# A two-layer hybrid encoder trunk: DeltaNet systems built one after each half projection, without TensorE transposes, and the triangular inverse written ahead of the mLSTM

## The chip, the cores and the metric

The kernel runs on one core of one Trainium2 chip. The metric is the device time of the whole program in microseconds (us), median of several runs. TensorE is PE in the profile (its weight loads PEld), VectorE DVE, ScalarE ACT, GpSimd POOL, and SyncE SP; SPq is the queue of DMA issues on SP.

## The reference

Input x is [1, 1024, 1024] in fp32. Two layers follow each other, each with an adaptive norm (`shift`, `scale`, `gate` from a matrix product of the conditioning vector with `ada_w`), one input projection, mixers and one output projection. The even layer's mixers are an mLSTM and a gated DeltaNet, each of four heads, forward and backward in time. Of the odd layer (convolution and dilated attention) nothing is changed. The DeltaNet part, where the change lies:

```python
a = strict_lower(beta * (k @ k^T) * exp(gc_i - gc_j))      # per chunk of 64 and head
tmat = a + eye
u = solve(tmat, beta * v);  w = solve(tmat, beta * exp(gc) * k)
attn = tril((q @ k^T) * exp(gc_i - gc_j))
for chunk in order:                                        # and once more, flipped in time
    v_new = u - w @ state
    o = (q * exp(gc)) @ state + attn @ v_new
    state = exp(gl) * state + (k * exp(gl - gc))^T @ v_new
```

## The kernel before, in words

All of x is held transposed, 128 rows by two halves of 512 tokens. A dense projection in fp32 is made of three matmuls in a reduced format: activations and weights are split in a high and a low part (`wsplit`: one load of 512 KB, a cast on ACT, a subtraction on POOL). `project` makes 128 output columns in two halves, and a half is 24 matmuls 128x512 (`prod`) into one of two PSUM banks set aside for that. These projections are named dq, dk, dv, mq, mk, mv, z.

**DeltaNet systems.** Time is cut in eight chunks of 128 tokens. `dn_system(ch)` makes the triangular system of a chunk, for four heads and two directions: four matmuls k·kᵀ into the bank KK (two such banks); a load of the table `gc_d` (cumulative log decays) spread over all 128 partitions; per direction a mask on POOL (L599), four exponentials on ACT (L624) and four multiplications on DVE (L647), and a store to `nd_d` in DRAM (L649). For the backward direction the blocks are transposed by TensorE into the bank NT (L158), copied by ACT (L655) and stored to `nt_d` (L656). All eight calls stand in a row in the program, ahead of the mlstm's buffers.

**Inverse.** `dn_inverse` loads the 64x64 blocks with one block in each partition, 64 for a direction (L675), inverts their 32x32 corners by 30 pairs of DVE steps (L681, L683), stores the result straight and with its axes swapped (ACT, L689), loads them as rows, and makes the corner blocks by products on PE (iG, iV, iT, with L706 on DVE ahead of the first). `dn_step`, the recurrence, reads what it stores: eight steps of two half-steps (one for each direction). A half-step is a chain of small matmuls (T1, T2, kS, Yr, qS, dS) with ACT and DVE between them. Where no projection is left to run beside it, PE waits in it.

**mLSTM.** `mlstm_weights(ch)` makes the scores S (PE, bank tag A), loads the table `nmu_d` spread over the partitions into E (L813), masks it, takes exponentials, multiplies by S (L818, DVE) and stores the product; `mlstm_step(j)` uses it. `m_k` also makes kw, keys by weights (L897).

**Beside it** runs `modulation`, a generator that reads `ada_w` piece by piece (L439 load of 256 KB, ACT L441, POOL L443); each `wsplit` moves it on by seven pieces, and after eight pieces PE sums the partitions (gps), with L456 on DVE behind.

**What sets the order.** The Tile framework's scheduler gives each engine one queue, filled in program order where nothing waits by its model; an engine runs its queue in order. `tc.issue_after(ins)` puts what is issued in it behind that instruction. The program's order is a list of steps, quoted with the change. After it come the recurrence with the rest of the projections, and the odd layer.

Of the kernel before, what the change touches and what calls it, by code (L numbers as in the profile page):

```python
# [9 lines left out]
F32 = mybir.dt.float32  # L10
# [7 lines left out]
P = 128  # L18
T = 1024
D = 1024  # L20
KT = 8
NCH = 8
# [34 lines left out]
def trunk(ctx, tc, x, c, norm_g, ada_w, ada_b, ev_w_in, ev_m_gate_b, ev_dn_dt_bias, ev_dn_a_log,  # L57
          ev_dn_conv_w, ev_m_norm_g, ev_dn_norm_g, ev_w_out, od_w_in, od_dw_w, od_dw_b, od_ln_g,
          od_ln_b, od_w_out, rel_bias, final_g, sel, onehot, seen, out):
    nc = tc.nc  # L60
# [8 lines left out]
    dr = pool("dr", 1, DRAM)  # L69
# [16 lines left out]
    def sl(off, *shape):  # L86
        return part_of(U, off, shape)

    def ring(off, n, *shape, of=None):

        size = 1
        for k in shape:
            size *= k
        i = 0
        while True:
            yield part_of(U if of is None else of, off + (i % n) * size, shape)
            i += 1
# [8 lines left out]
    def bank(name, shape=(P, 512), tag="t"):  # L106
        return psb.tile(list(shape), F32, tag=tag, name=name, bufs=BANKS[tag])
# [12 lines left out]
        tc.add_manual_dep(ins, first.name, mybir.DependencyInfo(mybir.DependencyClass.NoSync, mybir.DependencyReason.DATA),  # L120
                          reason="issue order")

    pace = {"gen": None, "n": 0}
    TICKS = 7
    uid = [0]

    def nm(s):
        uid[0] += 1
        return f"{s}_{uid[0]}"
# [26 lines left out]
    def tr(o, i):  # L156
        k = i.shape[0]
        nc.tensor.transpose(o, i, ident[:k, :k])  # L158
# [116 lines left out]
    def project(w, hT, name, use):  # L275
        for hf in range(2):
            ps = ibank(nm(name))
            prod(ps, w, hT[hf], range(KT))
            use(hf, ps)


    w0 = ev_w_in[0]
# [29 lines left out]
    def columns(g):  # L312
        for tiles, b0 in zip(ada[g], (2 * g, 8 + 2 * g)):
# [5 lines left out]
                          in_=wgr.rearrange("p k (g c) -> p k g c", g=4))  # L319
# [180 lines left out]
    cs1 = page("cs1", tag="a")  # L500
# [51 lines left out]
    nc.scalar.activation(out=wrow[0:8], in_=wrow[0:8], func=AF.Exp)  # L552
    nmu = cB
    nc.scalar.mul(out=nmu[0:8], in_=cs2[0:8], mul=-1.0)
    nmu_d = dr.tile([8, T], F32, name="nmu_d")
    wrow_d = dr.tile([8, T], F32, name="wrow_d")
    gc_d = dr.tile([8, T], F32, name="gc_d")
    wold_d = dr.tile([8, NCH], F32, name="wold_d")
    gl_d = dr.tile([8, NCH], F32, name="gl_d")
    nc.sync.dma_start(out=gc_d, in_=cs1[96:104])  # L560
    nc.sync.dma_start(out=nmu_d, in_=nmu[0:8])
    nc.sync.dma_start(out=wrow_d, in_=wrow[0:8])
    nc.sync.dma_start(out=wold_d, in_=wold)
    nc.sync.dma_start(out=gl_d, in_=tot[96:104])
# [1 line left out]
    for e in range(2):  # L566
        nc.sync.dma_start(out=woldb[e * 64:e * 64 + 64],
                          in_=wold_d.rearrange("(d q e) c -> e d q c", d=2, e=2)[e:e + 1].to_broadcast([64, 2, 2, NCH]))
# [6 lines left out]
    for src, dst in ((cs1, col1), (cs2, col2)):  # L575
        for q in range(2):
            b_ = turn(src, q)
            nc.vector.tensor_copy(out=dst[:, q * 4:q * 4 + 4, :].rearrange("p c (g r) -> p c g r", r=8),
                                  in_=b_.rearrange("p (c g r) -> p c g r", c=4, g=4)[:, :, :, 0:8])
# [20 lines left out]
                                channel_multiplier=cm_)  # L600

    def brow(src, d, ch):
        return src[4 * d:4 * d + 4, ch * P:(ch + 1) * P].rearrange("(o h) l -> o h l", o=1).to_broadcast([P, 4, P])

    cc = cst.tile([P, NCH, 8], F32, name="cc")
    ncc = cst.tile([P, NCH, 8], F32, name="ncc")
# [17 lines left out]
            nc.scalar.activation(out=B_[:, h, :], in_=B_[:, h, :], func=AF.Exp, bias=ngc[:, ch, 4 * d + h:4 * d + h + 1])  # L624

    nd_d = dr.tile([2, NCH, 4, P, P], F32, name="nd_d")
    nt_d = dr.tile([NCH, 4, P, P], F32, name="nt_d")

    xl_d = [dr.tile([2, 2, NCH, 4, 64, 64], F32, name=f"xl{i}_d") for i in range(2)]

    def etile(tag):
        return wk.tile([P, 4, P], F32, tag=tag, name=nm("E"), bufs=2)

    n_r, nt_r = ring(0, 4, 8, P), ring(4096, 2, 4, P)

    def dn_system(ch):
        tcs = slice(ch * P, ch * P + P)
        KK = bank(nm("KK"), (P, 4, P), "B")
        for h in range(4):
            mm(KK[:, h, :], kT[h][:, tcs], kT[h][:, tcs], True, True)  # L640
        B_ = next(n_r)
        nc.sync.dma_start(out=B_, in_=gc_d[:, tcs].rearrange("(o r) l -> o r l", o=1).to_broadcast([P, 8, P]))
        for d in range(2):
            decays(B_[:, 4 * d:4 * d + 4, :], d, ch)
            for h in range(4):
                u = 4 * d + h
                nc.vector.scalar_tensor_tensor(out=B_[:, u, :], in0=KK[:, h, :], scalar=ncc[:, ch, u:u + 1],  # L647
                                               in1=B_[:, u, :], op0=ALU.mult, op1=ALU.mult)
            nc.sync.dma_start(out=nd_d[d, ch].rearrange("h j i -> j h i"), in_=B_[:, 4 * d:4 * d + 4, :])  # L649

        ps = bank(nm("NT"), (P, 4, P), "A")
        for h in range(4):
            tr(ps[:, h, :], B_[:, 4 + h, :])
        Nt = next(nt_r)
        nc.scalar.copy(out=Nt, in_=ps)  # L655
        nc.sync.dma_start(out=nt_d[ch].rearrange("h i j -> i h j"), in_=Nt)  # L656

    def dn_inverse(n):

# [9 lines left out]
            return part_of(next(iv_r)[:, 0:n], 0, shape)  # L669

        sq = NL[:, 0:4096].rearrange("p (a b) -> p a b", b=64)
        for d, src in enumerate((nd_d[0], nt_d)):
            for b in range(2):
                bs = slice(64 * b, 64 * b + 64)
                nc.sync.dma_start(out=sq[64 * d + 32 * b:64 * d + 32 * b + 32],  # L675
                                  in_=src[:, :, bs, bs].rearrange("c h j i -> (c h) j i"))
        D2 = NL.rearrange("p (s x) -> p s x", s=2)[:, :, 0:2048].rearrange("p s (a b) -> p s a b", b=64)[:, :, :, 0:32]
        for k in range(30, 0, -1):
            m = 31 - k
# [23 lines left out]
        for ch in range(NCH):  # L703
# [3 lines left out]
            ps = bank(nm("iG"), (P, 4, 32), "C")  # L707
# [3 lines left out]
            ps = bank(nm("iV"), (P, 4, 32), "C")  # L711
# [78 lines left out]

    MARK = 1
    dn_scales()
    for ch in range(NCH):
        dn_system(ch)
    mq = [page(f"mq{j}", tag="a") for j in range(2)]
    mk = [page(f"mk{j}", tag="a") for j in range(2)]
    oml_d = dr.tile([NCH, P, 4, P], F32, name="oml_d")
# [124 lines left out]
                mlstm_weights(ch)  # L922
            mlstm_step(j)

    for step, n in ((dn_q, 0), (dn_v, 0), (m_q, 0), (dn_q, 1), (m_q, 1), (dn_q, 2), (dn_q, 3), (m_k, 1), (m_v, 0), (m_v, 2), (m_v, 3), (m_v, 1), (m_k, 0), (mlstm, 0), (dn_v, 1), (dn_inverse, 0), (gate_chunk, 0), (dn_v, 2), (gate_chunk, 1), (dn_v, 3)):
        step(n)
    Y_r, aux_r, ke_r, vv_r, v2_r = (ring(0, 2, 4, P), ring(1024, 2, 2, 4, 64), ring(2048, 2, 4, P), ring(3072, 3, 4, P),
                                    ring(5632, 2, 4, P))
# [677 lines left out]
```

## Time and profile before

| what | value |
|---|---|
| time of three runs | 1521.6, 1512.96, 1513.93 us; median 1513.93 |
| profiled execution | 1522.57 us, its span 1520.8 us |
| PE busy | 1344.9 us, 88% of the span |
| DVE, ACT, POOL busy | 879.0, 585.9, 460.4 us |
| granted TensorE clock, mean | 0.933 |

The span is what the profiler saw from the first to the last instruction. The granted clock is TensorE's, as a share of full speed: 1.00 is the upper of its two levels (2.4 GHz) all through a stretch, 0.50 the lower (1.2 GHz), and what lies between is a mixture. The program is one long PE queue with other engines beside it, so the stretches in which PE stands still or runs at the lower level are the ones to look at.

### The profile page before, as it was taken

To read this page: it belongs to the slowest core of one execution; us is meant where nothing else is said; L and a number is where in the kernel's file an instruction comes from. 1 tells how busy PE (TensorE), PEld (TensorE's weight loads), DVE (VectorE), ACT (ScalarE), POOL (GpSimd) and SP (SyncE) were. 2 spreads that over 40 slices of the span, in tenths; PEclk is the share of its full clock that TensorE was granted. 3 is DMA by queue.
4 is the path that set the end of the run, shared out by engine and by line. 5 is a ranking of instruction groups with operands and counts; after the bars stand their busy time and mean duration, and the time that the engine had idled before them with its cause. 6 is when DMAs were issued, how large, how long until landed. Compare 5 with 4: busy or idle time off the path is not lost. (4 is left out here: it accounts for less than half of the span.)

```text
span 1520.8 us, 20504 instructions
## 1 busy us (share of the span) xinstructions
PE 1344.9 (88%) x7331; PEld 1070.9 (70%) x7331; DVE 879.0 (58%) x1622; ACT 585.9 (39%) x1415; POOL 460.4 (30%) x357
## 2 busy tenths in 40 slices
PE   3978958878878988988999989889999999998998
PEld 2766746657667866777878857667776767876786
DVE  6789456933324641345854539998886454336334
ACT  5354454454444323343443321123324743326212
POOL 3454523444234511210234102322125233022210
PEclk9898987989899999889999999999999998997899
DMA  9334479369667785455655271010241233245322
GB/s 319 102 83 113 106 168 235 109 223 177 177 180 229 234 203 147 124 140 143 211 189 156 84 144 56 28 56 22 67 140 43 66 127 119 84 143 158 102 82 104
DMA packets 256456, 205.11 MB, mean 135 GB/s; under 512 B 59391, under 2 KB 219667, under 8 KB 256227
## 3 DMA queue, kind: packets, MB, share of 16 engines
q1 hardware_dynamic: 235555, 193.32, 45.1%
q10 hardware_dynamic: 20800, 10.49, 2.4%
q8 instruction: 58, 0.95, 0.3%
q14 instruction: 43, 0.35, 0.1%
HBM read 148.45 MB, written 58.98 MB: 136 GB/s over the span
## 5 line engine op out<-in xcount | busy, mean ns | idle before, releaser
L265 POOL TENSOR_TENSOR wlo<-wraw,whi 128x1024 fp32r<-128x1024 f32 x60 | 163.2, 2720 | 358.6 <-ACT whi L264 345.9
L1245 DVE SCALAR_TENSOR_TENSOR u<-xp,U,u 128x1009 f32<-128x1009 f32 (+14 forms) x120 | 176.2, 1502 | 1.0
L264 ACT CAST whi<-wraw 128x1024 fp32r<-128x1024 f32 x60 | 62.6, 1044 | 136.5 <-PE gb L139 49.1
L139 PE MATMUL z<-hhi,whi 128*128 128x512 f32 x256 | 108.1, 422 | 4.5 <-ACT mo L768 4.2
L139 PE MATMUL z<-hlo,whi 128*128 128x512 f32 x256 | 106.8, 417 | 0.0
L139 PE MATMUL z<-hhi,wlo 128*128 128x512 f32 x256 | 106.3, 415 | 0.0
L443 POOL TENSOR_TENSOR U<-U 128x512 f32<-128x512 f32 x56 | 79.4, 1419 | 76.9 <-ACT U L441 74.4
L139 PE MATMUL y<-wohi,mhi 128*128 128x512 f32 x240 | 97.9, 409 | 2.2 <-ACT mhi L1054 2.1
L139 PE MATMUL y<-wolo,mhi 128*128 128x512 f32 x240 | 96.8, 403 | 0.0
L139 PE MATMUL y<-wohi,mlo 128*128 128x512 f32 x240 | 96.1, 402 | 0.4 <-DVE mlo L1055 0.3
L441 ACT ACTIVATE U<-U,cs 128x512 f32<-128x512 f32 x64 | 45.9, 722 | 84.8 <-DMA U<-in_ada_w_dram 83.5
L599 POOL TENSOR_SCALAR_AFFINE_SELECT E<-E 128x512 f32<-128x512 f32 x32 | 21.4, 670 | 170.3 <-DMA E<-gc_d 71.3
L1397 DVE COPY U<-pT 128x512 f32<-128x512 f32 x48 | 32.5, 689 | 55.7 <-PE pT L158 55.6
L139 PEld LDWEIGHTS z<-hhi,whi 128*128 128x128 f32 x256 | 50.7, 198 | 16.7 <-ACT mo L768 4.6
L139 PEld LDWEIGHTS z<-hhi,wlo 128*128 128x128 f32 x256 | 50.5, 197 | 11.9 <-issue 1.1
L139 PEld LDWEIGHTS z<-hlo,whi 128*128 128x128 f32 x256 | 50.6, 197 | 11.3 <-issue 0.9
L139 PEld LDWEIGHTS y<-wohi,mhi 128*128 128x128 f32 x240 | 46.0, 192 | 13.5 <-ACT mhi L1054 2.5
L139 PE MATMUL sc<-ak,aq 128*128 128x256 f32 (+1 forms) x128 | 44.2, 429 | 11.6 <-DVE o L1372 9.8
L139 PEld LDWEIGHTS y<-wohi,mlo 128*128 128x128 f32 x240 | 45.9, 191 | 11.9 <-DVE mlo L1055 1.3
L1370 DVE CUSTOM_DVE_ANT_0 pt<-sc,U 128x256 f32<-128x256 f32 (+1 forms) x64 | 25.9, 404 | 48.6 <-PE sc L139 23.4
L139 PEld LDWEIGHTS y<-wolo,mhi 128*128 128x128 f32 x240 | 46.2, 193 | 10.3
L1374 ACT ACTIVATE pt<-pt,o 128x256 f32<-128x256 f32 (+1 forms) x64 | 31.4, 490 | 53.6 <-DVE o L1370 48.1
(455 smaller groups left out, 3603.7 us busy)
## 6 DMA issues: line engine op xcount, KB each, us to landing
wraw<-in_ev_w_in_dram SPq DMA_DIRECT2D x32, 512.0 KB
U<-in_ada_w_dram SPq DMA_DIRECT2D x64, 256.0 KB
wraw<-in_od_w_in_dram ACTq DMA_DIRECT2D x20, 512.0 KB
x<-in_x_dram SPq DMA_DIRECT2D x11, 512.0 KB
ada<-in_ada_w_dram SPq DMA_DIRECT2D x10, 512.0 KB
od_d<-o SPq DMA_DIRECT2D x64, 66.0 KB
U<-od_d SPq DMA_DIRECT2D x4, 1056.0 KB
U<-gc_d SPq DMA_DIRECT2D x8, 512.0 KB
```

The costliest lines, as they stand in the source:

```text
L139: return nc.tensor.matmul(o, lhsT=l, rhs=r, start=s, stop=e, skip_group_check=shared).ins
L264: nc.scalar.copy(out=hi, in_=raw)
L265: nc.gpsimd.tensor_tensor(out=lo, in0=raw, in1=f(hi), op=ALU.subtract)
L441: nc.scalar.mul(out=t_ if k else acc, in_=t_, mul=cs[:, k:k + 1])
L443: nc.gpsimd.tensor_tensor(out=acc, in0=acc, in1=t_, op=ALU.add)
L599: nc.gpsimd.affine_select(out=ap, in_=ap, pattern=[[0, 4], [pat, P]], compare_op=ALU.is_ge, fill=NEG, base=0, channel_multiplier=cm_)
L1245: nc.vector.scalar_tensor_tensor(out=y[:, lo:hi], in0=xp[:, lo + d:hi + d], scalar=w_, in1=y[:, lo:hi], op0=ALU.mult, op1=ALU.add)
L1370: nc.vector.tensor_tensor_reduce(out=x1_, in0=ps[:, c0:c1], in1=bias[:, e, c0:c1], scale=1.0, scalar=1e30, op0=ALU.add, op1=ALU.min, accum ...
L1374: nc.scalar.activation(out=x1_, in_=x1_, func=AF.Exp, scale=-1.0, bias=mn1, accum_out=o2[:, 0, 128 + e:129 + e])
L1397: nc.vector.tensor_copy(out=PT, in_=tb)
```

## The change

Four things change. (1) The eight `dn_system` calls no longer stand in a row. A new step `systems`, put behind the second mq projection, fills a list; `project` takes one system from it after each half projection and issues it behind that half's last matmul. (2) The backward transposes on PE, their copies on ACT and `nt_d` are gone. `dn_inverse` loads the backward blocks from `nd_d` in four rounds of two loads through one buffer `tmp`, and in each round a copy on ACT (64 partitions, 1024 elements in each) swaps the two axes of a block. The freed scratch space makes the ring of B_ five buffers instead of four. (3) The two tables `gc_d` and `nmu_d` are stored by chunk, so that what a load reads for one partition is one piece: 4 KB instead of eight of 512 B in `dn_system`, 2 KB instead of four of 512 B in the 32 loads of `brow` (16 of `nmu_d`, 16 of `gc_d`). (4) `dn_inverse` is written ahead of the mLSTM.

```diff
     def project(w, hT, name, use):
         for hf in range(2):
             ps = ibank(nm(name))
             prod(ps, w, hT[hf], range(KT))
             use(hf, ps)
+            if pace["sys"]:
+                with tc.issue_after(pace["mm"]):
+                    pace["sys"].pop(0)()
...
-    nmu_d = dr.tile([8, T], F32, name="nmu_d")
+    nmu_d = dr.tile([NCH, 8, P], F32, name="nmu_d")
...
-    gc_d = dr.tile([8, T], F32, name="gc_d")
+    gc_d = dr.tile([NCH, 8, P], F32, name="gc_d")
...
     def brow(src, d, ch):
-        return src[4 * d:4 * d + 4, ch * P:(ch + 1) * P].rearrange("(o h) l -> o h l", o=1).to_broadcast([P, 4, P])
+        return src[ch:ch + 1, 4 * d:4 * d + 4, :].to_broadcast([P, 4, P])
...
-    n_r, nt_r = ring(0, 4, 8, P), ring(4096, 2, 4, P)
+    n_r = ring(0, 5, 8, P)
...
-        nc.sync.dma_start(out=B_, in_=gc_d[:, tcs].rearrange("(o r) l -> o r l", o=1).to_broadcast([P, 8, P]))
+        nc.sync.dma_start(out=B_, in_=gc_d[ch:ch + 1].to_broadcast([P, 8, P]))
...
-        ps = bank(nm("NT"), (P, 4, P), "A")
-        for h in range(4):
-            tr(ps[:, h, :], B_[:, 4 + h, :])
-        Nt = next(nt_r)
-        nc.scalar.copy(out=Nt, in_=ps)
-        nc.sync.dma_start(out=nt_d[ch].rearrange("h i j -> i h j"), in_=Nt)
...
-        for d, src in enumerate((nd_d[0], nt_d)):
+        tmp = sl(4160, 16, 64)
+        for b in range(2):
+            bs = slice(64 * b, 64 * b + 64)
+            nc.sync.dma_start(out=sq[32 * b:32 * b + 32], in_=nd_d[0][:, :, bs, bs].rearrange("c h j i -> (c h) j i"))
+        for q in range(4):
             for b in range(2):
-                bs = slice(64 * b, 64 * b + 64)
-                nc.sync.dma_start(out=sq[64 * d + 32 * b:64 * d + 32 * b + 32],
-                                  in_=src[:, :, bs, bs].rearrange("c h j i -> (c h) j i"))
+                js = slice(64 * b + 16 * q, 64 * b + 16 * q + 16)
+                nc.sync.dma_start(out=tmp[64 + 32 * b:96 + 32 * b],
+                                  in_=nd_d[1][:, :, js, 64 * b:64 * b + 64].rearrange("c h j i -> (c h) j i"))
+            nc.scalar.copy(out=sq[64:128, :, 16 * q:16 * q + 16], in_=tmp[64:128].rearrange("p j i -> p i j"))
...
-    for ch in range(NCH):
-        dn_system(ch)
...
-    for step, n in ((dn_q, 0), (dn_v, 0), (m_q, 0), (dn_q, 1), (m_q, 1), (dn_q, 2), (dn_q, 3), (m_k, 1), (m_v, 0), (m_v, 2), (m_v, 3), (m_v, 1), (m_k, 0), (mlstm, 0), (dn_v, 1), (dn_inverse, 0), (gate_chunk, 0), (dn_v, 2), (gate_chunk, 1), (dn_v, 3)):
+    def systems(n):
+        pace["sys"] = [lambda ch=ch: dn_system(ch) for ch in range(NCH)]
+    for step, n in [(dn_q, 0), (dn_v, 0), (m_q, 0), (dn_q, 1), (m_q, 1), (systems, 0), (dn_q, 2), (dn_q, 3), (m_k, 1), (m_v, 0), (m_v, 2), (m_v, 3), (m_v, 1), (m_k, 0)] + [(dn_inverse, 0), (mlstm, 0), (dn_v, 1), (gate_chunk, 0), (dn_v, 2), (gate_chunk, 1), (dn_v, 3)]:
```

The first place is PE's queue among the systems, before the change (`128x128 x4` is four such instructions in a row; turn is a transpose of a projection's result):

```order
L158 MATMUL NT_1192<-ident,U 128x128 x4
L158 MATMUL turn_1465<-ident,qT_1456 128x128
L158 MATMUL NT_1229<-ident,U 128x128 x4
L139 MATMUL KK_1273<-kT_656 128x128
L139 MATMUL KK_1273<-kT_657 128x128
L139 MATMUL KK_1273<-kT_658 128x128
L139 MATMUL KK_1273<-kT_659 128x128
L158 MATMUL turn_1465<-ident,qT_1456 128x128 x3
L139 MATMUL KK_1310<-kT_656 128x128
L139 MATMUL KK_1310<-kT_657 128x128
L139 MATMUL KK_1310<-kT_658 128x128
L139 MATMUL KK_1310<-kT_659 128x128
```

Here KK and NT of successive systems follow each other with a few transposes of a projection's result between them. The same engine after the change, at the first system:

```order
L139 MATMUL dq_1696<-hlo_42_243,whi_1691 128x512
L139 MATMUL dq_1696<-hhi_38_239,wlo_1692 128x512
L139 MATMUL KK_1722<-kT_656 128x128
L139 MATMUL KK_1722<-kT_657 128x128
L139 MATMUL KK_1722<-kT_658 128x128
L139 MATMUL KK_1722<-kT_659 128x128
L139 MATMUL dq_1752<-hhi_43_244,whi_1691 128x512
L139 MATMUL dq_1752<-hlo_47_248,whi_1691 128x512
```

A group of KK now stands behind the last matmul of a half projection (`dq_1696`), and the next half (`dq_1752`) follows it; the eight groups stand so from the first half of the third dq to the second half of the first mv, and NT is gone.

The second place is DVE's queue in the inverse, before the change, from its last steps to the first product behind it:

```order
L681 TENSOR_TENSOR U<-U 128x60
L684 MEMSET U 128x64
L683 TENSOR_TENSOR U<-U 128x2x30
L220 TENSOR_TENSOR modc_106<-adaps_2018,vec 128x4
L897 TENSOR_TENSOR kw_2103<-turn_2098,kwf 128x512
L897 TENSOR_TENSOR kw_2106<-turn_2098,kwf 128x512
L897 TENSOR_TENSOR kw_2114<-turn_2109,kwf 128x512
L897 TENSOR_TENSOR kw_2117<-turn_2109,kwf 128x512
L706 TENSOR_TENSOR U<-U,diag_83 128x512
L220 TENSOR_TENSOR modc_106<-adaps_2278,vec 128x4
L818 TENSOR_TENSOR E_2534<-S_2528,E_2534 128x2x128
```

The chain L681/L683 ran to its end, then kw, then L706, and only then the mLSTM's multiplications (L818). After the change (those have become L816):

```order
L681 TENSOR_TENSOR U<-U 128x476
L816 TENSOR_TENSOR E_2717<-S_2711,E_2717 128x2x128
L816 TENSOR_TENSOR E_2729<-S_2711,E_2729 128x2x128
L816 TENSOR_TENSOR E_2717<-S_2712,E_2717 128x2x128
L816 TENSOR_TENSOR E_2729<-S_2712,E_2729 128x2x128
L683 TENSOR_TENSOR U<-U 128x2x14x17
L681 TENSOR_TENSOR U<-U 128x468
L683 TENSOR_TENSOR U<-U 128x2x13x18
L681 TENSOR_TENSOR U<-U 128x456
L683 TENSOR_TENSOR U<-U 128x2x12x19
L681 TENSOR_TENSOR U<-U 128x440
L683 TENSOR_TENSOR U<-U 128x2x11x20
```

Twelve of the 32 multiplications of the mLSTM now stand inside the chain, in three visits; each waits there for S and for its E, and the rest of the chain is queued behind it.

The third place is ACT's queue where the inverse's blocks are loaded, after the change (L676 is the copy that swaps axes, L904 empties an mv projection's bank, L444 is the modulation's, L264 the cast of `wsplit`):

```order
L904 COPY vT_2143<-mv_2176 128x512
L444 ACTIVATE U<-U,cs 128x512
L676 COPY U<-U 64x64x16
L444 ACTIVATE U<-U,cs 128x512
L904 COPY vT_2216<-mv_2249 128x512
L676 COPY U<-U 64x64x16
L444 ACTIVATE U<-U,cs 128x512 x2
L264 CAST whi_2392<-wraw_2391 128x1024
L904 COPY vT_2216<-mv_2275 128x512
L676 COPY U<-U 64x64x16
L444 ACTIVATE U<-U,cs 128x512 x2
L676 COPY U<-U 64x64x16
```

Before the change no copy of the inverse stood among the emptying of the mv banks at that place but those of L689; the four new copies, each of which waits for its round of loads, now do.

## Rows read from the trace of the kernel before

**Rows 1.** The page: its span, and busy time of the engines

```profile
span 1520.8 us, 20504 instructions
...
PE 1344.9 (88%) x7331; PEld 1070.9 (70%) x7331; DVE 879.0 (58%) x1622; ACT 585.9 (39%) x1415; POOL 460.4 (30%) x357
```

**Rows 2.** Windows: length, busy (count) of PE, PEld, DVE, ACT, POOL, clock, DMA

```profile
113.00:192.00 79.00, 73.14 (x319) 58.74 (x319) 56.03 (x53) 36.83 (x108) 37.92 (x28) 0.93 0.41 106
192.00:254.00 62.00, 39.25 (x182) 30.41 (x180) 36.04 (x88) 34.20 (x108) 12.24 (x16) 0.75 0.93 207
254.00:351.00 97.00, 82.19 (x353) 63.25 (x354) 57.41 (x77) 44.23 (x98) 46.01 (x33) 0.93 0.65 172
351.00:453.00 102.00, 82.91 (x421) 65.95 (x421) 36.94 (x73) 41.59 (x102) 39.48 (x35) 0.90 0.69 182
453.00:577.00 124.00, 108.39 (x666) 88.61 (x665) 59.15 (x161) 40.80 (x96) 46.82 (x50) 0.93 0.77 218
577.00:658.00 81.00, 75.58 (x437) 63.30 (x437) 24.33 (x52) 33.02 (x89) 16.07 (x17) 0.91 0.44 127
658.00:708.00 50.00, 40.04 (x276) 36.60 (x275) 20.75 (x57) 19.39 (x59) 4.89 (x11) 0.83 0.63 151
708.00:770.00 62.00, 60.41 (x454) 53.47 (x453) 47.78 (x127) 27.47 (x71) 13.27 (x11) 1.00 0.68 207
770.00:1520.00 750.00, 704.59 (x3899) 548.52 (x3898) 456.83 (x783) 254.42 (x617) 192.26 (x106) 0.96 0.32 96
```

**Rows 3.** What PE waited for, 192 to 254 us: total, times, longest

```profile
PE NT L158 <- ACT U L655: 9.5, 1, 9.5
```

**Rows 4.** Tile KK on PE: count, durations, first and last start, its waits

```profile
L139 PE MATMUL KK<-kT x64: 270/275/582, 113.0 to 219.3; 128*128 128x128 f32 x64
...
  DVE U L647: 5.7, 1
  DVE kT L403: 4.5, 1
```

**Rows 5.** Groups by line, 192 to 254 us: busy, mean ns, idle time before

```profile
L158 PE MATMUL NT<-ident,U 128*128 128x128 f32 x32 | 7.4, 360 | 12.6 <-ACT U L655 9.5 <-issue 3.0
...
L599 POOL TENSOR_SCALAR_AFFINE_SELECT U<-U 128x512 f32<-128x512 f32 x8 | 4.9, 634 | 25.9 <-DMA U<-gc_d 19.3 <-issue 3.6 <-DVE U L647 2.9
...
L655 ACT COPY U<-NT 128x512 f32<-128x512 f32 x8 | 4.4, 579 | 2.4 <-DMA nt_d<-U 2.4
```

**Rows 6.** Window of tile dk alone, dense projection

```profile
90.00:103.00 13.00, 13.00 (x58) 10.42 (x56) 0.57 (x1) 1.00 0.38 101
```

**Rows 7.** What PE waited for, 254 to 351 us

```profile
PE turn L158 <- DVE kw L897: 5.1, 1, 5.1
PE turn L158 <- DVE grow L456: 3.7, 1, 3.7
```

**Rows 8.** What PE waited for, 351 to 453 us

```profile
PE S L139 <- DVE E L818: 10.5, 4, 2.9
```

**Rows 9.** Timeline, 387 to 393 us: a 256 KB row load, its reader

```profile
387.16 0.38 SPq L813 DMA_DIRECT2D E<-nmu_d  x1
...
392.29 0.64 POOL L599 TENSOR_SCALAR_AFFINE_SELECT E<-E 128x512 f32<-128x512 f32 x1 [8.87 <-DMA E<-nmu_d]
```

**Rows 10.** Timeline, 291 to 295 us: a 256 KB weight load, its reader

```profile
291.28 0.33 SPq L439 DMA_DIRECT2D U<-in_ada_w_dram  x1
...
294.00 0.72 ACT L441 ACTIVATE U<-U,cs 128x512 f32<-128x512 f32 x1 [1.12 <-DMA U<-in_ada_w_dram]
```

**Rows 11.** DVE timeline, 261 to 347 us: inverse's first step, first block product

```profile
262.00 0.25 DVE L681 TENSOR_TENSOR U<-U 128x60 f32<-128x60 f32 x1
...
346.65 0.69 DVE L706 TENSOR_TENSOR U<-U,diag 128x512 f32<-128x512 f32 x1 [16.37 <-DMA U<-xl_d]
```

**Rows 12.** Groups by line, 254 to 360 us: copies that swap two axes

```profile
L689 ACT COPY U<-U 128x512 f32<-128x512 f32 x8 | 8.8, 1111 | 16.2 <-DVE U L683 9.3 <-DMA xl_d<-U 6.8
```

**Rows 13.** Windows of tile Yr on PE, 658 to 708 us

```profile
658.00:708.00 50.00, 6.37 (x32) 0.83 0.63 151
```

More of the change, by code (lines that the diff above doesn't have):

```diff
@@ L121, in behind @@
                           reason="issue order")
-    pace = {"gen": None, "n": 0}
+    pace = {"gen": None, "n": 0, "sys": []}
     TICKS = 7
@@ L554, in trunk @@
     nc.scalar.mul(out=nmu[0:8], in_=cs2[0:8], mul=-1.0)
-    nmu_d = dr.tile([8, T], F32, name="nmu_d")
+    nmu_d = dr.tile([NCH, 8, P], F32, name="nmu_d")
     wrow_d = dr.tile([8, T], F32, name="wrow_d")
-    gc_d = dr.tile([8, T], F32, name="gc_d")
+    gc_d = dr.tile([NCH, 8, P], F32, name="gc_d")
     wold_d = dr.tile([8, NCH], F32, name="wold_d")
     gl_d = dr.tile([8, NCH], F32, name="gl_d")
-    nc.sync.dma_start(out=gc_d, in_=cs1[96:104])
-    nc.sync.dma_start(out=nmu_d, in_=nmu[0:8])
+    nc.sync.dma_start(out=gc_d.rearrange("c r l -> r c l"), in_=cs1[96:104].rearrange("r (c l) -> r c l", l=P))
+    nc.sync.dma_start(out=nmu_d.rearrange("c r l -> r c l"), in_=nmu[0:8].rearrange("r (c l) -> r c l", l=P))
     nc.sync.dma_start(out=wrow_d, in_=wrow[0:8])
@@ L626, in trunk @@
     nd_d = dr.tile([2, NCH, 4, P, P], F32, name="nd_d")
-    nt_d = dr.tile([NCH, 4, P, P], F32, name="nt_d")
     xl_d = [dr.tile([2, 2, NCH, 4, 64, 64], F32, name=f"xl{i}_d") for i in range(2)]
```

## The prediction

> **What bounds the kernel now.** I read the page first: PE is busy for 1344.9 of 1520.8 us [rows 1]. A dense half projection is 24 matmuls, and where they run without a break 58 take 13.00 us, 0.22 us each at clock 1.00 [rows 6], so about 5.4 us a half. PE is the bound nearly everywhere, and what a change of order can win is time in which PE stands still or runs at the lower clock. So I cut the span into windows and work out for each the lost time: its length less PE's busy time, plus (1 − clock) times the busy time [rows 2]. That is rough, since a slower clock stretches only what PE does, but it says where to look:
>
> 113–192: 5.9 + 5.1 = 11.0; 192–254: 22.8 + 9.8 = 32.6; 254–351: 14.8 + 5.8 = 20.6; 351–453: 19.1 + 8.3 = 27.4; 453–577: 15.6 + 7.6 = 23.2; 577–658: 5.4 + 6.8 = 12.2; 658–708: 10.0 + 6.8 = 16.8; 708–770: 1.6. Together 145 us. Behind 770 the change moves next to nothing on PE; I leave that part as it is, within 3.
>
> In 192–254 the waits name one long stop: PE stands 9.5 us before a transpose NT, until ACT's copy of an earlier NT has freed the bank [rows 3]. The groups say what ACT waited for in turn: the masks on POOL stood 19.3 us for the loads of `gc_d`, and the copies 2.4 us for the stores of `nt_d` [rows 5]. This is the block of systems: dense projections stand behind it in PE's queue, and the clock is 0.75. In 254–351 PE waits for kw and for the modulation's row (5.1 and 3.7) [rows 7], in 351–453 mainly for the mLSTM's products, S before E (10.5 in four stops) [rows 8]. In 658–708 the chain of half-steps has no projection beside it: 32 matmuls Yr are eight groups of four, which with two for a step of both directions is eight half-steps, and PE is busy for 40.04 of 50 at clock 0.83 [rows 13, 2].
>
> The forecast is the sum of the changes, made against the profiled execution, 1522.57 us. The median, 1513.93, lies 8.6 below that and the three runs 0.6% apart, so 1% (15 us) is about what a measurement of this kernel can tell from no change.
>
> **NT goes.** 32 transposes at 360 ns on average are busy 7.4 us together (they overlap in pairs) [rows 5]. All are on PE's queue in the block. Some of that is in waiting already counted below, so I take **−4**; bounds −7.4 and 0. ACT loses eight copies (4.4 us) that nobody but NT waited for.
>
> **113–192.** The KK matmuls waited 4.5 us once for kT and 5.7 us once for a bank that the decays on DVE still held [rows 4]. The first KK now stands behind the first half of the third dq. The convolution and its transposes that fill the rest of this stretch stay, so I take **−5** of 11.0; bounds −9 and 0.
>
> **192–254, the main term.** KK is followed by a half projection instead of the next system. A system needs its load, two masks, eight exponentials and eight multiplications. Eight of them passed in this window, 62/8 = 7.8 us each at most, with a PE half of 5.4 us. KK has two banks, so a system may take two halves, 10.9 us, before PE waits for the bank. The loads of `gc_d` too have five buffers in place of four, so they can go out earlier. I keep 10 us lost (modulation's sums wait for pieces that queue on SP behind the stores of `nd_d`, and these remain) and win **−22**. Bounds: −32.6 if nothing is lost, and +20 if each of eight systems stops PE for 2.5 us.
>
> **254–351.** The kw and the grow wait (8.8) belong to an order that is gone; I expect a third of them back: **−6**. Here lies the new work of the inverse. Of the old swap (L689, eight copies) one takes 1.11 us for 512 elements [rows 12], so a copy of 1024 elements is some 2.2 us, four 8.9 us. They stand in ACT's queue between the copies that empty the mv banks, and each waits for its round of two loads; `tmp` is one buffer, so round, copy, round follow each other. A round's price is not in the trace; the nearest rows are a 256 KB load in pieces of 512 B, 5.1 us from issue to its reader [rows 9], and one in pieces of 2 KB, 2.7 us [rows 10]. Four rounds are 4 × (2.7 + 2.2) = 19.6 to 4 × (5.1 + 2.2) = 29.2 us. I take the upper, as 256 B pieces are nearer to the first row. If a copy waits 3 to 4 us at the head of ACT's queue, the mv copies behind it wait too and PE has two banks in hand: bounds −15 and +15.
>
> Does the inverse become late? Before, from the last KK (219.3) to its first DVE step (262.0) it took 42.7 us [rows 4, 11], and in that lay the block's last systems, NT, its copy, store and loads. Now the last system is alone; the rounds come in place of NT's way. I keep 42.7. From the first step to the first block product another 84.7 us [rows 11]. After the change the order puts 455 matmuls of 512 columns and 101 others on PE between the last KK and the first iG. At 0.22 us and, for the others, some 0.17 (an estimate from KK's 0.27 [rows 4], of which neighbours overlap), with 20 us of waiting as in this window before, that is 137 us, against 42.7 + 84.7 = 127 us: the inverse is ready about **10 us before** PE asks. So it costs nothing, narrowly.
>
> **351–453.** The inverse is ahead of the mLSTM, and between the first and last S now stand 310 wide matmuls, not 206: 104 × 0.22 = 23 us more to cover E's chain (load, mask, exponentials, product). The E loads get shorter, if 2 KB pieces bring them from 5.1 to 2.7 us [rows 9, 10]. Ten of the stops' 10.5 us go, and with them part of the lower clock and of the later waits for the mLSTM's products: 27.4 to 12, **−15**; bounds 0 and −20. 453–577 keeps its work: **−1**.
>
> **577–770, what is given back.** The projections moved up are missing at the end. By the order eight half-steps now have no projection beside them, against five before. The eight of [rows 13] lose 16.8 us in 50, part of them covered; over four that stand wholly bare this is 4.2 each, so three more cost 12.6. `gc_d` is loaded for the half-steps in quicker pieces, less 3: **+10**; bounds +4 and +17.
>
> **Sum.** −4 − 5 − 22 − 6 − 15 − 1 + 10 = −43: 1522.57 − 43 = 1479.6 for an execution like the profiled, and by the 8.6 between that and the median **1471**.
>
> **The rule on small pieces.** The traced loads of equal size took 5.1 us in 512 B pieces and 2.7 in 2 KB pieces [rows 9, 10], with other work on the queues. The Trainium skill ("DMA: Bandwidth & Descriptors", Specifications) gives 512 B as the smallest transfer for line rate; by that, the tables before were already at it, the new layout is worth nothing, and it names a result of its own (rival c).
>
> **Rivals.**
>
> (a) *The inverse decides.* Three visits of the mLSTM's multiplications now stand inside DVE's chain; each waits for its E, and the chain behind it too. If E's load, mask and four exponentials keep the chain for as long as the eight visits lay apart before (102 us for seven gaps, 14.6 each [rows 2]), three are 44 us, less the 10 in hand: iG some 30 us late. For it: DVE is in order, and L706 stood idle 16.4 for its rows already [rows 11]. Against: E is loaded well ahead, as the ring has two tags of two. 30 late gives about **1501**.
>
> (b) *Slower: eight small stops for one block.* Spread out, each system breaks up a run of dense matmuls. If a system's way through load, POOL, ACT and DVE, with the convolutions and the mv copies in the same queues, takes longer than the two halves that KK's banks allow (10.9 us), PE stops after every half. At 10 us of stop and lower clock a system this is 80 instead of the 32.6 of the block, +47 in place of −22: **1540**. The point from which it decides is 10.9 us a system; the old bound, 7.8, speaks against it, the stops of 19.3 us for `gc_d` and 9.5 behind them [rows 3, 5] for it.
>
> (c) *The tables bring nothing.* Loads of E and of `gc_d` stay at 5.1 us: 4 of the 15 in 351–453 and the 3 in the half-steps are missing, +7: **1478**.
>
> (d) *All is hidden.* Nothing is lost in 192–254 (−10 more), the mLSTM's window is as clean as 708–770 (−10) and half the loss at the end is covered (−5): **1446**.
>
> That the change doesn't do what it says is excluded: the order shows KK one by one behind the halves.
>
> **Chances.** The forecast .41, (a) .18, (b) .11, (c) .15, (d) .15. The range takes in (a), (c), most of (d) and a part of the way to (b), where a milder form of either late chain ends: 1432 to 1518. Faster by over 1% (below 1499): forecast, (c), (d) and a part of (a), together .77; within 1% the rest of (a) and a mild (b), .12; slower the rest, .11.
>
> **What would show it.** In the trace after: no wait of PE for NT, groups of KK some 5 to 7 us apart with a clock near 1.00 between them (if 10 or more, and PE waiting for KK's bank on DVE, it is (b)). The four copies of L676 with 5 us or less of idle each before them, and no wait of an mv matmul for L904. iG and iT without waits; a wait of PE for the first block products on DVE of 20 us or more is (a). E loads near 2.7 us from issue to mask (near 5: (c)). Waits S before E under 4 us together. At the end eight bare half-steps, each losing about 4 us. The prediction is wrong if the gain in 192–254 comes back as waits for the sums of the modulation, whose pieces stand on SP behind the stores, or if the bare half-steps cost 8 and not 4 each.

## The result, and the profile after

The changed kernel takes 1439.65 us (1434.67 to 1443.33, four runs), the kernel before 1513.88: a ratio over all runs of 0.9499, 95% interval 0.9461 to 0.9537, or 74 us less. Forecast were 43 less. The profiled execution took 1441.71 us, 80.9 under that of before; its page begins so (to be held against [rows 1]):

```profile
span 1439.9 us, 20401 instructions
...
PE 1319.2 (92%) x7299; PEld 1049.9 (73%) x7299; DVE 881.4 (61%) x1622; ACT 589.2 (41%) x1411; POOL 471.8 (33%) x357
```

The windows of the changed kernel, cut where the same matmuls stand in both kernels (first mk, first and last S, first T, first y; columns as in [rows 2]):

```profile
113.00:187.00 74.00, 66.85 (x283) 53.54 (x284) 57.51 (x57) 37.90 (x115) 41.26 (x29) 0.89 0.43 120
187.00:230.30 43.30, 35.19 (x162) 26.80 (x160) 25.40 (x48) 29.96 (x94) 20.39 (x16) 0.86 0.55 159
230.30:318.10 87.80, 82.53 (x380) 66.48 (x380) 40.01 (x78) 44.88 (x95) 42.95 (x32) 0.95 0.65 168
318.10:431.80 113.70, 102.88 (x510) 81.01 (x510) 71.74 (x116) 57.65 (x120) 51.30 (x41) 0.95 0.80 228
431.80:543.10 111.30, 104.29 (x665) 84.93 (x663) 50.08 (x154) 36.84 (x96) 39.70 (x45) 0.97 0.79 234
543.10:702.30 159.20, 148.92 (x1098) 130.30 (x1098) 95.49 (x241) 78.37 (x223) 35.55 (x41) 0.97 0.65 198
702.30:1440.00 737.70, 700.90 (x3873) 545.56 (x3873) 458.39 (x773) 250.48 (x602) 188.29 (x103) 0.96 0.31 95
```

The same matmuls of the kernel before start at 254.1, 350.8, 453.5, 576.8 and 775.9 us. Where the order moved dense matmuls from one stretch to another, I take them out at 0.225 us each (between the 0.22 of [rows 6] and the 0.235 that the clock lets through on average):

| stretch | before | after | matmuls moved | net | forecast |
|---|---|---|---|---|---|
| 113 to first mk | 141.1 | 117.3 | 0 | −23.8 | −31 |
| first mk to first S | 96.7 | 87.8 | 0 | −8.9 | −6 |
| first to last S | 102.7 | 113.7 | +104 | −12.4 | −15 |
| last S to first T | 123.3 | 111.3 | −15 | −8.6 | −1 |
| first T to first y | 199.1 | 159.2 | −89 | −19.9 | +10 |
| first y to the end | 744.9 | 737.7 | 0 | −7.2 | 0 |

Small matmuls are not taken out: four of the eight groups of KK, 1.05 us busy each, now stand behind the first mk, so some 4 us of the gain in the first line belong to the second.

So far it looks like a forecast that held in front and missed at the end, where 20 us were won and not 10 lost. The end names the cause. Timeline of the kernel before, one load of a half-step and the mask that reads it, and then the same of the changed kernel:

```profile
584.22 0.38 SPq L975 DMA_DIRECT2D E<-gc_d  x1
...
589.17 0.64 POOL L599 TENSOR_SCALAR_AFFINE_SELECT E<-E 128x512 f32<-128x512 f32 x1 [9.70 <-DMA E<-gc_d]
```

```profile
585.47 0.33 SPq L977 DMA_DIRECT2D E<-gc_d  x1
...
589.37 0.63 POOL L602 TENSOR_SCALAR_AFFINE_SELECT E<-E 128x512 f32<-128x512 f32 x1 [8.25 <-DMA E<-gc_d]
```

5.0 us from issue to mask against 3.9. That is one of 40 loads. Over all, the median from issue to mask fell from 11.5 to 5.9 us for the 8 loads of the systems, from 6.4 to 4.9 for the mLSTM's 16 and from 5.9 to 4.1 for the half-steps' 16. (A mask can also wait for POOL's other work in that time.) The theory to be tried (M) is that the layout of the two tables, not the order, made most of the gain; the rival (R), that the order did and the tables were worth the few us of the prediction.

### The profile page after: what moved, and what is told of

The parts are those of the page before. It is cut to its first block, busy times and chain, and to the rows that moved or that the text cites. A ratio compares the mean times of both kernels' runs of the same rounds, so it can differ in the third digit from the quotient of the medians.

```text
span 1439.9 us, 20401 instructions
## 1 busy us (share of the span) xinstructions
PE 1319.2 (92%) x7299; PEld 1049.9 (73%) x7299; DVE 881.4 (61%) x1622; ACT 589.2 (41%) x1411; POOL 471.8 (33%) x357
## 4 chain that ended last, share of the span: by engine, by line
PE 59%; DVE 15%; DMA 15%; ACT 4%; SPq 3%; issue 3%; POOL 2%; POOLq 0%; ACTq 0%; DVEq 0%
PE y L139 12%; PE z L139 8%; PE sc L139 4%; DVE u L1247 4%; PE ob L139 3%; PE gb L139 3%; PE dq L139 2%; PE av L139 2%; PE pT L158 2%; PE ak L139 2%; PE mo L139 2%; PE mq L139 2%; PE aq L139 2%; PE ga L139 2%; DVE U L212 1%
## 5 line engine op out<-in xcount | busy, mean ns | idle before, releaser
L264 ACT CAST whi<-wraw 128x1024 fp32r<-128x1024 f32 x60 | 62.7, 1046 | 131.0 <-PE gb L139 46.3
L139 PE MATMUL z<-hhi,whi 128*128 128x512 f32 x256 | 104.2, 407 | 0.0
L139 PE MATMUL z<-hlo,whi 128*128 128x512 f32 x256 | 103.9, 406 | 0.0
L444 ACT ACTIVATE U<-U,cs 128x512 f32<-128x512 f32 x64 | 46.1, 723 | 66.6 <-DMA U<-in_ada_w_dram 64.2
L139 PEld LDWEIGHTS z<-hhi,wlo 128*128 128x128 f32 x256 | 48.7, 190 | 11.5 <-issue 0.8
L139 PEld LDWEIGHTS y<-wohi,mlo 128*128 128x128 f32 x240 | 45.6, 190 | 11.5 <-DVE mlo L1057 0.9
```

Source lines behind the costliest of these rows:

```text
L139: return nc.tensor.matmul(o, lhsT=l, rhs=r, start=s, stop=e, skip_group_check=shared).ins
L264: nc.scalar.copy(out=hi, in_=raw)
L444: nc.scalar.mul(out=t_ if k else acc, in_=t_, mul=cs[:, k:k + 1])
```

## The experiments

Ratios are to the kernel before, run beside it on the same chip; a difference of 0.01 is 15 us. Differences to the changed kernel are taken from the ratios; by the intervals, a difference between two runs is uncertain by some 7 us.

**tab: the kernel before, with the tables alone.** The edit is the part of the change's diff that touches `nmu_d`, `gc_d`, `brow` and the load of B_.

> The kernel before with the two re-laid tables alone. Theory M (the half-steps at the end lost their time to slow loads of gc_d on SP, which also held the masks of the systems and of the mLSTM): 1474 to 1494 us, about 30 under the kernel before, of which some 15 between the first T and the first y, 10 in the block of systems, 5 at the waits S before E. Rival R (the end got quicker by the order, since the inverse's rows are stored earlier; the tables are worth the 4 and 3 us of the prediction): 1505 to 1512. The rule that 512 B pieces are at line rate already: 1514, no change.

1458.75 us, 0.9627 (0.9584 to 0.9670): 56 us less, twice what M expected. NT, the systems in a row and the mLSTM ahead of the inverse are all still there. The block's groups of tab show what became of the masks:

```profile
L599 POOL TENSOR_SCALAR_AFFINE_SELECT U<-U 128x512 f32<-128x512 f32 x8 | 5.3, 691 | 12.6 <-DVE U L647 11.6 <-issue 1.0
```

In [rows 5] the same masks stood 25.9 us, 19.3 of them for the loads of `gc_d`; here none for a load. PE's wait in that block, 9.5 us in [rows 3], shrank with it:

```profile
PE NT L158 <- ACT U L655: 4.7, 1, 4.7
```

So about half of the wait at NT was only the end of a chain that began with a slow load.

**notab: the changed kernel with the tables of before.** The same lines, taken back.

> The changed kernel with the two tables laid as before (512 B pieces). M: 1460 to 1480, some 20 to 40 over the changed kernel, at least half of it between the first T and the first y (159 us in the changed kernel, 175 or more here). R: 1440 to 1449 and that stretch within 5 us of 159.

1497.33 us, 0.9887 (0.9851 to 0.9924), 59 us over the changed kernel, more than M allowed; from the first T to the first y it takes 181.0 us where the changed kernel takes 159.2. PE's waits in notab from 578 to 700 us begin with a copy on ACT (L960, in whose queue the exponentials stand that wait for the masks) and with a load:

```profile
PE T L139 <- ACT U L960: 12.0, 2, 9.6
PE T L139 <- DMA U<-xl_d: 5.1, 2, 3.8
```

The systems, NT, the ACT swap and the order together are worth 17 us without the tables and, by 0.9627 to 0.9499, 19 with them. R has fallen as the main cause, and so has the view that 512 B pieces were good enough wherever they lie.

**gsys, gbrow, nmu: one use of the tables at a time**, in the kernel before. For `gc_d` a second table in the new layout is stored beside the old; the load of B_ in `dn_system` is gsys's, that in `dn_step` gbrow's, that of E nmu's, and `brow2` is the new form of `brow`; for nmu, `nmu_d` itself is re-laid:

```diff
+    gc2_d = dr.tile([NCH, 8, P], F32, name="gc2_d")
...
-        nc.sync.dma_start(out=B_, in_=gc_d[:, tcs].rearrange("(o r) l -> o r l", o=1).to_broadcast([P, 8, P]))
+        nc.sync.dma_start(out=B_, in_=gc2_d[ch:ch + 1].to_broadcast([P, 8, P]))
...
-                    nc.sync.dma_start(out=B_, in_=brow(gc_d, d_, ch))
+                    nc.sync.dma_start(out=B_, in_=brow2(gc2_d, d_, ch))
...
-            nc.sync.dma_start(out=E, in_=brow(nmu_d, d, ch))
+            nc.sync.dma_start(out=E, in_=brow2(nmu_d, d, ch))
```

> The kernel before, with only the loads of the systems (U from gc_d) from a re-laid table; the other loads stay as before. If the 57 us of both tables come use by use, each where its load is waited for: about 1500 (1494 to 1505), the gain of some 17 between the first KK and the first S, and the rest of the program as before. If they come from less traffic on the DMA queues as a whole: 8 of 40 such loads, 8 of 16 MB, about 1488.

1498.79 us, 0.9883 (0.9849 to 0.9917). The first S starts at 331.9 and not at 350.8 us; the stretch of S and that behind T stay as long as before (103.4 and 197.3 us).

> The kernel before, with only the half-steps' loads (E from gc_d) from a re-laid table. Use by use: about 1500 (1495 to 1505), the gain of some 16 between the first T and the first y. Traffic as a whole: 4 of 16 MB, about 1503, but spread over other stretches too. If the half-steps were held by the inverse's rows (R): 1510 or more.

1501.28 us, 0.9895 (0.9862 to 0.9928). Windows from the first T to the first y, first of the kernel before, then of gbrow, with the same 1187 matmuls in both:

```profile
576.80:775.90 199.10, 180.42 (x1187) 156.09 (x1187) 98.10 (x244) 83.93 (x236) 37.46 (x41) 0.92 0.58 165
```

```profile
570.20:751.50 181.30, 175.12 (x1187) 151.34 (x1187) 98.23 (x244) 83.56 (x236) 37.28 (x41) 0.95 0.60 182
```

17.8 us less for the same order of the same work: PE idles 6.2 us and not 18.7, at a higher clock.

> The kernel before, with only the mLSTM's loads (E from nmu_d) from a re-laid table. Use by use: about 1497 (1490 to 1502), the gain of some 17 between the first and the last S, and 5 behind it. If the waits S before E were DVE's and not the loads': 1510 or more.

1488.82 us, 0.9815 (0.9782 to 0.9848), a little more gain than was expected. From first to last S it takes 83.3 us and not 102.7, and of the stops of S for E [rows 8] one is left. The tile S on PE in nmu (count, durations, first and last start), and PE's wait there:

```profile
L139 PE MATMUL S<-mq,mk x64: 272/272/374, 343.9 to 427.2; 64*128 64x128 f32 x64
```

```profile
PE S L139 <- DVE E L821: 1.9, 1, 1.9
```

Another 7 us of nmu's gain lie ahead of the first S (343.9 and not 350.8), where two of its 16 loads are issued among the systems.

18 + 16 + 28 us make 62, against 56 for all at once: use by use, each mostly where its load was waited for.

**pad and pitch: why the old layout was slow.** Pieces of 512 B again, 528 B apart (pad, first below, in the new layout) or 4224 B apart (pitch, in the old layout with 32 more elements in a row), `nmu_d` likewise; both edits are made in the changed kernel, and pitch takes the loads of the kernel before:

```diff
-    gc_d = dr.tile([NCH, 8, P], F32, name="gc_d")
+    gc_d = dr.tile([NCH, 8, P + 4], F32, name="gc_d")
...
-    gc_d = dr.tile([NCH, 8, P], F32, name="gc_d")
+    gc_d = dr.tile([8, T + 32], F32, name="gc_d")
```

> The changed kernel with four unused elements behind each row of 128 in the two tables, so that a partition's read is again made of pieces of 512 B, but only 528 B apart and not 4096 as in the kernel before. If the size of the pieces is what counts: as slow as the changed kernel with the old tables, 1480 to 1500. If it is how far apart they lie: 1435 to 1450.

1453.24 us, 0.9578 (0.9543 to 0.9613): 12 us over the changed kernel and 3 above the second answer's range, far from the first's.

> The changed kernel with the two tables laid as before, but with 32 unused elements behind each row of 1024: pieces of 512 B that lie 4224 B apart and not 4096. If it is the distance of 4096 B as such (a power of two) that makes the loads slow: 1448 to 1460, as with pieces 528 B apart. If it is that the pieces lie far apart at all: 1485 to 1500, as with the tables of before.

1469.14 us, 0.9684 (0.9645 to 0.9723), between the two answers: 28 us over the changed kernel, 31 under notab. So of the tables' 59 us some 31 come from the distance of exactly 4096 B, 16 from the pieces' lying far apart at all and 12 from what pad and the changed kernel still differ in: the pieces' size, and that pad's pieces start off a multiple of 512 B, which no run takes apart. One load of a system in pitch and the masks that read it, from its timeline:

```profile
200.29 0.36 SPq L644 DMA_DIRECT2D U<-gc_d  x1
...
205.69 2.79 POOL L602 TENSOR_SCALAR_AFFINE_SELECT U<-U 128x512 f32<-128x512 f32 x2 [2.16 <-DMA U<-gc_d]
```

That is 5.4 us. Over the eight, issue to mask in the median: 9.7 us in notab, 6.5 in pitch, 5.9 in pad, 5.9 in the changed kernel. For E's loads, of four pieces and not eight, it is another matter: 6.8, 6.3, 5.7 and 4.9 us for the mLSTM's in the same four kernels, and 6.1, 5.6, 4.7 and 4.1 for the half-steps'. So the step from 4096 to 4224 B helps the systems above all, and 17 of its 28 us (spans of the profiled executions) are won before the first mk, of notab and of pitch:

```profile
L139 PE MATMUL mk<-hhi,whi x32: 392/400/793, 249.0 to 336.1; 128*128 128x512 f32 x32
```

```profile
L139 PE MATMUL mk<-hhi,whi x32: 392/399/796, 231.8 to 319.0; 128*128 128x512 f32 x32
```

**row: the systems in a row again**, `dn_system` called in a loop ahead of mq, all else as changed.

> The changed kernel with the eight systems in a row ahead of mq and mk again (tables, ACT swap and order stay). If the block's loss was the row itself (no dense matmuls between systems): 1454 to 1468, with 15 us or more of PE idle or at a lower clock between 187 and 250 us over the changed kernel. If it was NT and the slow tables (the waits named there): 1436 to 1447, since both are gone here.

1451.79 us, 0.9579 (0.9550 to 0.9608): 12 us over the changed kernel and just under the first of the two ranges. The window of the block:

```profile
187.00:250.00 63.00, 48.34 (x211) 37.18 (x210) 44.89 (x96) 44.20 (x119) 20.75 (x25) 0.81 0.81 209
```

By the measure of the prediction 14.7 + 9.2 = 23.9 us are lost here, in the changed kernel's 187 to 230.3 only 8.1 + 4.9 = 13.0. From 113 to 187 row loses less (5.1 + 4.8 against 14.5), and its first S starts at 328.0 where the changed kernel's starts at 318.1: up to there the row costs 10 us even with quick loads and without NT.

**nt: the transposes on PE again**, with `nt_d`, its copies and stores, and four buffers of B_.

> The changed kernel with the backward blocks transposed by TensorE again (32 transposes, 8 copies and 8 stores of 256 KB; four buffers of B_, not five), systems still one after each half projection, tables re-laid. By the prediction's term for NT (4, at most 7.4 us on PE): 1443 to 1449. If the four rounds of loads and copies that came in its place cost what they save: 1436 to 1442. If the spread systems need NT gone (its bank and its copies on ACT between the mv banks): 1452 or more.

1443.86 us, 0.9508 (0.9469 to 0.9547): not to be told from the changed kernel. The first S comes 7.8 us later (325.9), the first iG 25 us earlier (383.0 and not 408.0).

**order: the mLSTM ahead of the inverse again.**

```diff
-    ... [(dn_inverse, 0), (mlstm, 0), (dn_v, 1), (gate_chunk, 0), (dn_v, 2), (gate_chunk, 1), (dn_v, 3)]:
+    ... [(mlstm, 0), (dn_v, 1), (dn_inverse, 0), (gate_chunk, 0), (dn_v, 2), (gate_chunk, 1), (dn_v, 3)]:
```

> The changed kernel with the mLSTM written ahead of the inverse again. M: 1446 to 1458; the waits S before E come back in part (some 5 to 10 us), and the stretch from the first T to the first y loses 15 to 25 matmul-us of cover less, so that it stays as quick per half-step (bare half-steps of 6 to 9 us). R: 1460 or more, with waits of T for the inverse's rows (U<-xl_d) of 8 us or more as in the kernel before.

1455.18 us, 0.9589 (0.9552 to 0.9627): 14 us over the changed kernel. The size is M's, the place is R's. What PE waits for in it at S, 318 to 432 us, and then from 430 to 582 us, up to the half-steps:

```profile
PE S L139 <- DVE E L816: 0.7, 2, 0.4
```

```profile
PE T L139 <- DMA U<-xl_d: 12.0, 1, 12.0
```

No stops of S came back; the first T waits 12 us for the inverse's rows. Taken back one at a time, the row, NT and the order come to 12 + 1 + 14 = 27 us, where all of them together are 17 to 19; whether they overlap or the difference is noise stays open.

**relay: more tables off powers of two.** Of these `wrow_d` too is read by many partitions at once: each of its loads gives 64 of them the same two pieces, 8 KB apart before the edit.

```diff
-    wrow_d = dr.tile([8, T], F32, name="wrow_d")
+    wrow_d = dr.tile([NCH, 8, P], F32, name="wrow_d")
...
-    nd_d = dr.tile([2, NCH, 4, P, P], F32, name="nd_d")
+    nd_d = dr.tile([2, NCH, 4, P + 1, P], F32, name="nd_d")[:, :, :, 0:P, :]
...
-    xl_d = [dr.tile([2, 2, NCH, 4, 64, 64], F32, name=f"xl{i}_d") for i in range(2)]
+    xl_d = [dr.tile([2, 2, NCH, 4, 66, 64], F32, name=f"xl{i}_d")[:, :, :, :, 0:64, :] for i in range(2)]
```

> The changed kernel, with more tables taken off distances that are powers of two: the mLSTM's old weights (wrow_d, 28 loads of two pieces 8 KB apart) laid by chunk, and the blocks of nd_d and of the inverse's rows (xl_d) one or two rows further apart (64 KB + 512 B, 16 KB + 512 B). If such distances slow those loads and stores too and PE waits for them in the stretch from S to the last half-step: 1418 to 1434. If only the broadcast tables suffer, which all partitions read at once: 1436 to 1443.

1442.94 us, 0.9499 (0.9445 to 0.9554): nothing. Nor did these loads get shorter: from the second load of a pair to its reader `wrow_d` takes 4.7 us in the median in the changed kernel and 5.5 in relay. POOL's waits for it over the whole program, in the same order:

```profile
POOL U L833 <- DMA U<-wrow_d: 41.2, 5, 11.8
```

```profile
POOL U L833 <- DMA U<-wrow_d: 43.9, 6, 12.4
```

ACT's waits for `nd_d` at L676 are 9.5 and 9.1 us. So no cost of these distances is seen; one is shown only for the 4096 B between the pieces of the two tables.

**mix: convolutions spread**, an attempt at a better version: dq, mq, dv, mq, systems, dq, mv, dq, mk, dq, then as changed.

> The changed kernel with projections that need a convolution and those that don't in turn (dq, mq, dv, mq, then the systems behind dq, mv, dq, mk), in place of five with one in the first seven. In the changed kernel PE waits 8.6, 4.8 and 2.3 us for convolutions and their followers between 104 and 150 us. If DVE's queue of convolutions holds PE between 104 and 230 us, spreading them gives back 8 to 15 us: 1425 to 1432, a kernel that beats both. If the waits only move to where the convolutions now lie: 1436 to 1450.

1453.43 us, 0.9582 (0.9550 to 0.9614), 13 us slower than the changed kernel and above both answers' ranges. The wait of 8.6 us for kT stayed (8.7), and a new one came between 187 and 215 us, for squares on ACT behind a convolution:

```profile
PE turn L158 <- ACT junk L411: 12.8, 1, 12.8
```

No version here beats the changed kernel.

## Why the prediction was right, and where it was not

The time, 1439.65, lies in the range (1432 to 1518), the side is right, and it is nearest to rival (d), at 1446, though not by (d)'s reasons: 13.0 us are still lost from 187 to the first mk, and 16.0 between the first and the last S (10.8 idle, 5.1 by the clock). The reasons of the forecast were right in part only, and that the time lies in the range is in good part luck. Without its tables terms the forecast was −36 (43 less the 7 of rival (c)); the same without the tables measured −17 (notab). The tables, priced at 7, made up for that and for the step that follows.

**The step that failed: "577–770, what is given back", +10; it was −20.** It took the loss of a half-step, 4.2 us, to come from having no projection beside it, and priced three more of them at 12.6. Three more there are (the first eight half-steps have four bare ones before and seven after), and with the old tables the price holds too. The seven in notab lose 21.7 us idle and 8.7 by the clock, 4.3 each:

```profile
609.20:685.40 76.20, 54.47 (x433) 50.13 (x432) 30.28 (x86) 31.68 (x94) 10.70 (x18) 0.84 0.57 138
```

But the half-steps beside a projection lost too, and in both kinds it was mostly a load. gbrow shows it: with the order untouched, quicker loads of `gc_d` give 17.8 us in the stretch, and half of that in three half-steps that have projections beside them. Those of the kernel before, then of gbrow, with the same 272 matmuls:

```profile
591.30:646.40 55.10, 50.39 (x272) 41.70 (x273) 15.87 (x31) 20.39 (x51) 11.18 (x11) 0.91 0.42 119
```

```profile
584.30:630.50 46.20, 46.20 (x272) 38.23 (x271) 15.83 (x31) 19.87 (x51) 10.93 (x11) 1.00 0.47 137
```

They lost 4.7 + 4.5 = 9.2 us, 3.1 each, so a half-step that loses its projection costs about 1 us more, and not 4.2: from the first T to the first y notab is 1.9 us longer than the kernel before, moved matmuls taken out. The sign was in [rows 2]: 708–770 lost only 1.6 us, although its last three half-steps are bare as well. Only the first eight half-steps load `gc_d`; the others load finished blocks from DRAM.

```profile
755.70:769.00 13.30, 11.75 (x107) 10.89 (x106) 10.21 (x33) 4.01 (x14) 1.34 (x2) 1.00 1.02 308
```

In the changed kernel the window of bare half-steps is this, against 658 to 708 in [rows 2]:

```profile
577.00:629.00 52.00, 48.26 (x405) 44.61 (x406) 29.39 (x85) 25.93 (x79) 7.21 (x15) 0.91 0.64 184
```

3.7 + 4.3 = 8.1 us lost in nearly seven half-steps (53 Yr), 1.2 each. The step also misread its row: a matmul of fp32 stands as two instructions in the trace (32 KK in the order are 64 in [rows 4]), so 32 Yr are four half-steps and not eight; the price of 4.2 each was the right one all the same.

**The tables**, which the prediction priced at 7 us (rival (c)) inside other terms, measured 56 to 59. The rows for it were there: 19.3 us of POOL's wait for `gc_d` [rows 5] and 5.1 against 2.7 us [rows 9, 10]. I read the first as a detail of the block and the second as a saving of 2.4 us a load. But E has two buffers of a kind, so load, mask, exponentials and product follow each other in a loop, and what a load takes longer comes back at each of the half-steps' 16 loads, two in each of the first eight; the systems' 11.5 us were not looked up at all. The loop is read from the code, and the waits along it bear it out. From the first T to the first y, POOL's masks wait for the load and ACT's exponentials for the masks, in the kernel before and then in gbrow:

```profile
POOL E L599 <- DMA E<-gc_d: 71.3, 10, 12.8
...
ACT E L624 <- POOL E L599: 45.7, 13, 10.6
```

```profile
POOL E L601 <- DMA E<-gc_d: 49.7, 10, 9.4
...
ACT E L629 <- POOL E L601: 24.9, 10, 6.8
```

The price was also read from one load: 5.1 us [rows 9] is one of the shortest of the mLSTM's 16, whose median is 6.4. So the sign named for rival (c), loads of E near 5 us from issue to mask, came (4.9 in the median) although (c) was wrong.

**192–254, −22 (with −4 for NT and −5 ahead of it).** Measured −23.8 for the three, where 31 were forecast. The cause was shared: gsys gives 18 by the loads alone, row 12 by the spread. NT is worth 1 by the ratio of nt, 4 by its median, both within the interval and inside its bounds of 0 to 7.4. The −5 for 113–192 did not come: 14.5 us are lost in 113 to 187, by 7.2 idle and the clock of 0.89, with waits for the convolutions.

**254–351, −6**, measured −8.9, or some −13 with the four groups of KK that came into it. The four copies took 2.0 us each, 0.2 under the estimate, and waited 9.5 us in all for their rounds. Their rows of the changed kernel, by line:

```profile
L676 ACT COPY U<-U x4: 1909/2032/2064, 280.0 to 298.4; 64x1024 f32<-64x1024 f32 x4
its engine sat idle before it (us, times) until:
  DMA U<-nd_d: 9.5, 4
```

The inverse began at 300.3 us, 39.4 after the last KK (42.7 forecast). **Rival (a) did not come**: DVE's first block product stands at 400.8, PE's iG at 408.0 and without a wait, so some 6 us are in hand where 10 were forecast. Its mechanism did show, in a smaller size: with the mLSTM's multiplications inside, the way from the first step to the first block product took 100.5 us and not 84.7, 16 more where (a) put 44, and PE too asked later than forecast (147 us after the last KK, not 137). On DVE:

```profile
300.31 0.25 DVE L681 TENSOR_TENSOR U<-U 128x60 f32<-128x60 f32 x1 [10.23 <-ACT U L676]
...
400.82 0.68 DVE L706 TENSOR_TENSOR U<-U,diag 128x512 f32<-128x512 f32 x1
```

**351–453, −15**, measured −12.4, but not for the reason given. More dense matmuls between the S groups were to cover E's chain. order has the mLSTM ahead again and S waits 0.7 us there; nmu takes 19.4 us out of the stretch with the old order. The loads had to get shorter; the cover was not needed. What the order is worth (14 us) it earns where the prediction looked for nothing, in the inverse's rows being stored before the first T asks (453–577: −8.6, forecast −1).

**Rival (b)** had its condition, 10.9 us a system and PE waiting for KK's bank, and it was not met: the 64 instructions of KK are eight groups, 9.6 us from one to the next in the mean (five gaps of 6.9 to 7.7 us, two of 13.0 and 18.7). That is more than the 5 to 7 expected, but dense matmuls stand between them and KK waits for nothing. The old bound of 7.8 us a system was misread: all eight NT pass in 192–254, but the masks of only four systems, 8 of 16 [rows 5].

```profile
L139 PE MATMUL KK<-kT x64: 272/275/377, 192.5 to 260.9; 128*128 128x128 f32 x64
```

**Rival (c) is refuted** by tab. The Trainium skill ("DMA: Bandwidth & Descriptors", Specifications) has 512 B as the smallest transfer at line rate; pad agrees in the main (at most 12 of 59 us hang on the size), but the pieces of before were slow for where they lay. The same page of the Trainium skill ("Latency and other measured facts") measures a slowdown for rows whose distance is a large power of two, from 2 MiB up, and little at 512 KiB (207 of 214 GB/s), for one long piece in each partition. No run here has such distances; here a cost shows at 4 KiB, in loads by which every partition reads the same pieces, by notab against pitch.

**Open** is the last row of the table: the 7 us between the first y and the end. All runs with the ACT swap or the inverse ahead take 734 to 740 us there, all made from the kernel before 740 to 747. The matmuls there are the same in number (3873 in both) and in PE's busy time (700.4 and 700.9 us); what is gone is idle time, and no run tells why.

## What to carry to other kernels

A load that one engine waits for in a loop is priced by its time on the queue, every visit: look up each load from its issue to its reader before pricing an order by the matmuls beside it. Where PE waits at the end of a chain (a transpose, a product), follow the chain back to the load; the engine named is only the last. Where every partition reads the same table, store what one read wants in one piece, and where that can't be, keep the pieces close, or at least off the 4096 B that was slow here; for other powers of two no such cost was seen.

## What was not expected of the hardware

For a read by which all partitions get the same pieces, pieces of 512 B cost by where they lie: with 4096, 4224 and 528 B between their starts, and in one piece of 2 or 4 KB, the same program took 1497, 1469, 1453 and 1440 us. The step away from 4096 B shows most in loads of eight pieces (9.7 to 6.5 us from issue to reader), little in those of four (6.8 to 6.3 and 6.1 to 5.6).
